# Swapping the banks of two accumulators, and tying two weight casts behind a copy, in the feed-forward of a two-layer trunk

## The chip, the cores and the metric

The kernel runs on one core of a Trainium2 chip. The metric is the device time of one execution in microseconds (us), lower is better. TensorE (PE) multiplies matrices into PSUM, ScalarE (ACT) and VectorE (DVE) work on SBUF and PSUM, and loads are issued by SyncE (SP) and GpSimd (POOL). Each engine takes its own instructions in order and waits for the others through semaphores.

## The reference

A trunk of two residual layers over 512 tokens of 1024 features in float32. Each layer adds a token mixer (layer 0 pools over windows, layer 1 is attention) and then a gated feed-forward; a last norm follows.

```python
for i in range(DEPTH):                                  # 2
    x = x + mixer_i(rmsnorm(x, norm_mix[i]))
    h = rmsnorm(x, norm_ffn[i])                         # (512, 1024)
    g = h @ ffn_w_gate[i]                               # (512, 2816)
    u = h @ ffn_w_up[i]
    x = x + (silu(g) * u) @ ffn_w_down[i]
return rmsnorm(x, norm_final)
```

## The kernel before

**Precision.** A float32 product is done in three passes of a narrower format. A weight tile is cast by ScalarE to its high part (`whi`, line 171), and VectorE subtracts it to get the rest (`wlo`, line 175). Tokens are held in the same two parts. A product is whi times the high tokens, whi times the low tokens, and wlo times the high tokens.

**Feed-forward by seven products.** The 2816 gate and up features are taken in groups of 256 of each, n = 0 to 10. A group is split by two into halves of features, of inputs and of tokens, and done with seven products (i = 0 to 6) of combined blocks where the plain way takes eight. `Group.product(i)` (line 696) gets the weights of product i, issues its matmuls, and then has the sums handled by `done` or `paired_done`. After the last of its products a group applies silu and multiplies gate and up (`gate_first`, line 767), and splits the result into parts `u_hi` and `u_lo` (`first_half`, `second_half`) for the down products. The down products (`Down`) are done in seven products too, for blocks of 3, 3 and 5 groups.

**Order of the work.** TensorE's order is written by hand in `PLAN`. Groups 0 and 1 go first, interleaved (`TWO`). Then come groups 2 to 10, the paired ones. Group 2's products go in the order 0, 2, 3, 1, 4, then product 0 of group 3, then 5 and 6 of group 2, and so on. From group 3 on, product 0 of a group is thus followed by products of other work, while group 2's product 0 is followed at once by its product 2. The order on ScalarE, VectorE and the load queues is chosen by a planner. It takes what is ready by its own reckoning, earlier program order first, and `high_priority` moves work forward. `issue_after(ins)` places an instruction behind `ins` on the same engine.

**Weights.** All weight operands of the kernel stand in one list, `queue`, in the order of their enqueuing; group 2's products 0, 1, 2, 3, 4 stand there in that order, followed by product 0 of group 3. `weights(i)` (line 151) issues loads up to five or ten operands ahead and casts and subtractions up to `split_ahead` operands ahead (four unless the caller says otherwise), as far as the five buffers of `whi` and `wlo` allow. Raw weights have five buffers (`wraw`) and three more for sums (`vraw`). Some operands are sums: a subtraction can be followed by VectorE additions (`then`, line 177) that form the raw weights of a later product. An entry `cast_behind` in an operand's item ties its cast (line 171) behind an instruction of ScalarE.

**PSUM banks.** There are eight. Groups 0 and 1 use four banks of the pool `mm` and four of the pool `ffps`, of which two belong to the sums p and two to the sums r. When product 6 of group 1 has been issued, both pools are closed and four tensors of two banks each take their place, `pair0` to `pair3`:

```python
fps.open("ffpairs", [P, 2, S], 1)
*A, Q, C = (fps.tile(f"pair{i}") for i in range(4))
```

`pair0` and `pair1` (A, used in turn by the groups) lie where `mm` was, `pair2` where p was, `pair3` where r was. An instruction that first writes a new tensor waits for the last reader of what lay there before.

**The copies.** Products 0, 2, 4 and 6 of a paired group go into its A tensor. After product 0 ScalarE copies A to Q (line 739, "first copy", kept as `self.kept`), so that product 2 can add to A while product 3 adds to Q. After product 2 it copies A to C (line 741), to which products 1 and 5 ("second products") add. Products 0, 2, 3, 5 and 6 have eight matmuls of 512 columns and eight of 256; products 1 and 4 have 24 of 256. The last reader of p before the change of pools is line 793, in product 6 of group 1; the last reader of r is line 789, in its product 5.

Of the kernel before, what the change touches and what calls it, by code (L numbers as in the profile page):

```python
# [75 lines left out]
def trunk_kernel(ctx: ExitStack, tc: tile.TileContext, x_in, xT, gam, gains, consts, ident_d, w0, wT, w1, wv, w_down, out):  # L76
# [37 lines left out]
    queue = []  # L114
# [26 lines left out]
    def load_sums():  # L141

        done = loaded["v"]
        for i in range(len(ready), min(len(queue), len(ready) + 20)):
            if queue[i]["kind"] == "v" and "src" in queue[i] and i not in raws:
                if "v" not in pools or len(done) >= V_TILES and queue[done[-V_TILES]]["last"] >= len(ready):
                    return
                load(i)
                done.append(i)

    def weights(i, split_ahead=4, load_ahead=5, held=0):

        load_ahead = queue[i].get("ahead", load_ahead)
        for n in range(loaded["w"], min(len(queue), i + load_ahead)):
            if queue[n]["kind"] == "w":
                load(n)
            loaded["w"] = n + 1
        load_sums()
        while len(ready) < min(loaded["w"], i + split_ahead):
            item = queue[len(ready)]  # L160
            if item["kind"] == "v" and "v" not in pools:
                break
            if "pool" not in item and len(ready) > i and held + sum("pool" not in it for it in queue[i : len(ready)]) >= RING:
                break
            shape = item["shape"]
            n = math.prod(shape)
            raw = raws[item.get("into", len(ready))]
            hi, lo = (pools.get(item.get("pool"), wspl).tile([P, 1024], F32R, name=item.get("pool", "w") + part) for part in ("hi", "lo"))
            if len(ready):
                with tc.issue_after(item["cast_behind"]) if "cast_behind" in item else nullcontext():  # L170
                    nc.scalar.copy(hi[:, :n], raw[:, :n])  # L171
            else:
                nc.vector.tensor_copy(hi[:, :n], raw[:, :n])
            with tc.issue_after(item["behind"]) if "behind" in item else nullcontext():
                nc.vector.tensor_sub(lo[:, :n], raw[:, :n], hi[:, :n].bitcast(F32))  # L175
            for into, more in item.get("then", ()):
                nc.vector.tensor_add(raws[into][:, :n], raws[into][:, :n], raws[more][:, :n])  # L177
            if "loads" in item:
                into, src = item["loads"]
                nc.gpsimd.dma_start(raws[into][:, :n].rearrange("p (k c) -> p k c", k=shape[0]), src, accum_op=ALU.add)  # L180
            if len(shape) == 2:
                ready.append(tuple(t[:, :n].rearrange("p (k m) -> p k m", k=shape[0]) for t in (hi, lo)))
            else:
                ready.append(tuple(t[:, :n].rearrange("p (g k m) -> p g k m", g=shape[0], k=shape[1]) for t in (hi, lo)))
        got = ready[i]
        ready[i] = None
        return got
# [280 lines left out]
    with ExitStack() as pctx:  # L468
# [5 lines left out]
        held = ExitStack()  # L474
# [20 lines left out]
        for c in range(NC):  # L495

            pieces = (slice(0, P), slice(P, S)) if c == 0 else (slice(0, S),)
            if c < 2 or c % 2 == 0:
                if c < 2:
                    load_x(c, pieces[0])  # L500
                whi, wlo = weights(j_in[0][c if c < 2 else 1 + c // 2], 1, 1)
# [7 lines left out]
            k = 0 if c < 2 else c % 2  # L509
# [98 lines left out]
    def ffn(layer, norm, third, nxt):  # L608
# [7 lines left out]
        gu, dn = j_ffn[layer]  # L616
        with ExitStack() as fctx:
# [19 lines left out]
            fps = Sums()  # L637
# [21 lines left out]
            held = ExitStack()  # L659
# [3 lines left out]
            class Group:  # L663
# [30 lines left out]
                    split(hi[:, 2:7, :], lo[:, 2:7, :], lst[:, 3:8, :])  # L694

                def product(self, i, held=0):
                    whi, wlo = weights(gu[self.n][i], held=held)
                    right = RIGHT[i]
                    if self.pairs:
                        a, q, c = self.pairs  # L700
                        to = (a, c, a, q, a, c, a)[i]
                        places = [(g, k) for g in range(2) for k in range(4)]
                        mat = lambda o, w, m, **kw: nc.tensor.matmul(o, lhsT=w, rhs=m, skip_group_check=True, **kw)  # L703
                        own = lambda g: to[:, g, HALVES[i == 1]]
                        if i in (1, 4):
                            for g, k in places:
                                mat(own(g), whi[:, g, k, :], right[:, 0, k, :], start=False, stop=False)
                                mat(own(g), whi[:, g, k, :], right[:, 1, k, :], start=False, stop=False)
                                mat(own(g), wlo[:, g, k, :], right[:, 0, k, :], start=False, stop=k == 3)
                        else:  # L710
                            for g, k in places:
                                both = to[:, g, :].rearrange("p (z c) -> p z c", z=2)
                                mat(both, whi[:, g, k, :], right[:, :, k, :], start=i == 0 and k == 0, stop=False)
                            for g, k in places:
                                mat(own(g), wlo[:, g, k, :], right[:, 0, k, :], start=False, stop=k == 3)
                        with tc.high_priority(URGENT if i < 5 else 100):
                            self.paired_done(i)
                        return
                    if i == 3:
                        self.sums["q"] = by_g(mm.tile())  # L720
                    elif i < 2:
                        self.sums["pr"[i]] = by_g(fps.tile("pr"[i]))
                    ps = self.sums["prpqprp"[i]]
                    for g in range(2):
                        for c in range(4):
                            for k, (w, z) in enumerate(((whi, 0), (whi, 1), (wlo, 0))):
                                nc.tensor.matmul(  # L727
                                    ps[:, g, :], lhsT=w[:, g, c, :], rhs=right[:, z, c, :],
                                    start=i in (0, 1, 3) and g + c + k == 0, stop=c == 3 and k == 2, skip_group_check=True,
                                )  # L730
                    with tc.high_priority(URGENT if i < 5 else 100):
                        self.done(i)
# [139 lines left out]
            groups = {0: Group(0, ct_common), 1: Group(1, ct_tile(hn, "ct_second"))}  # L872
# [4 lines left out]
            for at, (kind, n, i, *zs) in enumerate(PLAN[:-4]):  # L877
                if at in (0, 2):
                    b = 2 + at // 2
                    if b == 2:  # L880
                        late_banks[b] = third
                        norm.prepare(3, COLS)
                    else:
                        late_banks[b] = [r_tile(), by_four(mm.tile())]
                        for half in range(2):
                            norm.turn(b, half, late_banks[b][half])
                    late(b, 1)
                if at in (4, 6, 8):
                    for b in (2, 3):
                        late(b, at // 2)  # L890
                if kind == "down":
                    if n not in downs:
                        downs[n] = Down(n, A[0], C, Q)
                        A.reverse()
                    downs[n].product(i, *zs)
                    continue
                if kind == "quad" and i == 0:
                    groups[n] = Group(n, ct_common, (A[0], Q, C))
                    A.reverse()
                elif i == 0 and n not in groups:  # L900
                    groups[n] = Group(n, ct_common)
                groups[n].product(i, held={1: -2, 2: 1, 3: 1}.get(i, 0) if kind == "quad" else 0)
                if (n, i) == (2, 0):
                    with tc.high_priority(100), tc.issue_after(groups[2].kept.ins):
                        groups[1].second_half()
                    held.close()
                    late_u.append(open_pool("ffb", 2))
                if (n, i) == (1, 6):
                    fps.close()
                    mm.close()  # L910
                    fps.open("ffpairs", [P, 2, S], 1)
                    *A, Q, C = (fps.tile(f"pair{i}") for i in range(4))
                    A.reverse()


# [64 lines left out]
        return norm  # L980

    norm = ffn(0, norm, third, 1)


    with ExitStack() as actx:
# [179 lines left out]
        for t in range(8):  # L1165
# [4 lines left out]
            k = rope(pk, t, "k")  # L1170
# [115 lines left out]
        for part in range(2):  # L1286
            at = VA + part * VB
            pv = [mm.tile([P, S], F32, name="mm") for _ in range(4)]
            for c in range(4):
                whi, wlo = weights(j_v[part][c])  # L1290
# [137 lines left out]
```

## Time and profile before

| | |
|---|---|
| median of 3 runs | 990.42 us (990.29, 990.42, 991.89) |
| the profiled execution | 992.42 us, its span 990.6 us |
| TensorE busy | 975.5 us, 98% of the span |
| VectorE busy | 785.5 us, 79% |
| ScalarE busy | 580.5 us, 59% |
| mean granted TensorE clock | 0.991 |

The span is the time from the first to the last record of the execution. Rows of a timeline give the start, the duration, the engine, the line of the kernel, the operation, output<-inputs and the shapes; in square brackets stands the idle time of the engine before it and what ended it. "x8" joins eight instructions to one row. Instructions of one engine overlap by some tens of ns in the rows, so that the distance from one start to the next (the pitch) is shorter than the duration. A row of stretches gives the busy time of TensorE, its weight loads, VectorE, ScalarE and GpSimd, then the granted TensorE clock, the DMA share and GB/s.

### The profile page before, as it was taken

The page shows a single profiled execution, that of the slowest core. Times are in us where ns is not written, and L with a number is a line of the kernel's source. Part 1 is how long each engine was busy: PE and PEld are TensorE (multiplying, and loading weights), DVE is VectorE, ACT ScalarE, POOL GpSimd, SP SyncE. Part 2 cuts the span into 40 slices and gives each one's busy share as a digit, 9 for nine tenths or more (in the row PEclk, how much of TensorE's full clock was granted, in tenths as well). Part 3 has the DMA queues.
Part 4 walks back from the last instruction along what each step waited for, and adds up shares of the span by engine and source line. Part 5 has one row for each costly group of instructions (what it writes and reads, how often), then busy time and mean ns, then how long its engine had stood idle before and what let it go on. Part 6 is the DMA issues. An engine that isn't in the chain of part 4 may idle for free.

```text
span 990.6 us, 15451 instructions
## 1 busy us (share of the span) xinstructions
PE 975.5 (98%) x5948; PEld 862.3 (87%) x5948; DVE 785.5 (79%) x1085; ACT 580.5 (59%) x909; POOL 124.8 (13%) x124
## 2 busy tenths in 40 slices
PE   9999998999999999999999999999899999999997
PEld 8888897988988998889888899899788998899886
DVE  6485798897888888697897557589789798888876
ACT  5563665655665666574553554467564676567655
POOL 0002010011011111101211124101001101111110
PEclk9999998999999999999999999999899999999999
DMA  9448275379668876655221249617547956987652
GB/s 333 182 164 197 43 203 151 113 197 241 171 149 214 228 206 150 126 192 162 85 78 54 62 154 279 121 64 204 133 128 200 253 138 156 247 225 191 142 135 107
DMA packets 79465, 162.98 MB, mean 165 GB/s; under 512 B 6096, under 2 KB 6480, under 8 KB 79392
## 3 DMA queue, kind: packets, MB, share of 16 engines
q1 hardware_dynamic: 58544, 122.04, 37.3%
q0 software_dynamic: 20560, 39.69, 23.6%
q8 instruction: 46, 0.75, 0.3%
q14 instruction: 27, 0.22, 0.1%
q10 hardware_dynamic: 288, 0.27, 0.1%
HBM read 159.85 MB, written 2.13 MB: 164 GB/s over the span
## 4 chain that ended last, share of the span: by engine, by line
PE 96%; DVE 3%; ACT 1%; issue 0%; ACTq 0%
PE pair L703 36%; PE pair L845 21%; PE mm L264 5%; PE mm L266 4%; PE mm L265 4%; PE p L727 3%; PE early L515 2%; PE mm L425 2%; PE mm L427 2%; PE mm L426 2%; PE r L727 2%; PE mm L727 1%; PE mm L1296 1%; PE mm L1298 1%; PE mm L1297 1%; PE early L562 1%
## 5 line engine op out<-in xcount | busy, mean ns | idle before, releaser
L175 DVE TENSOR_TENSOR wlo<-wraw,whi 128x1024 fp32r<-128x1024 f32 (+2 forms) x190 | 221.7, 1172 | 68.7 <-ACT whi L171 68.2
L171 ACT CAST whi<-wraw 128x1024 fp32r<-128x1024 f32 (+2 forms) x189 | 183.9, 979 | 137.5 <-PE pair L703 29.1
L171 ACT CAST whi<-vraw 128x1024 fp32r<-128x1024 f32 (+1 forms) x108 | 105.2, 980 | 124.0 <-PE pair L703 40.9
L175 DVE TENSOR_TENSOR wlo<-vraw,whi 128x1024 fp32r<-128x1024 f32 (+1 forms) x108 | 121.5, 1133 | 56.9 <-ACT whi L171 52.2
L703 PE MATMUL pair<-h,whi 128*128 128x512 f32 (+1 forms) x720 | 161.1, 349 | 0.0
L703 PEld LDWEIGHTS pair<-h,whi 128*128 128x128 f32 x720 | 122.7, 189 | 15.0
L703 PE MATMUL pair<-t,whi 128*128 128x512 f32 (+1 forms) x576 | 128.0, 344 | 7.7 <-ACT pair L739 7.7
L703 PEld LDWEIGHTS pair<-t,whi 128*128 128x128 f32 x576 | 98.8, 194 | 18.2 <-ACT pair L739 8.1
L845 PE MATMUL pair<-wlo,u_hi 128*128 128x512 f32 (+1 forms) x284 | 110.0, 387 | 0.0
L845 PE MATMUL pair<-whi,u_hi 128*128 128x512 f32 (+1 forms) x284 | 109.9, 387 | 0.0
L845 PE MATMUL pair<-whi,u_lo 128*128 128x512 f32 (+1 forms) x284 | 109.8, 386 | 0.0
L703 PE MATMUL pair<-h,wlo 128*128 128x256 f32 x576 | 100.3, 281 | 0.0
L703 PEld LDWEIGHTS pair<-h,wlo 128*128 128x128 f32 x576 | 85.6, 188 | 4.7
L703 PE MATMUL pair<-t,wlo 128*128 128x256 f32 x432 | 82.2, 287 | 0.0
L138 POOL DMA_DIRECT2D wraw<-w x22 | 26.6, 1211 | 395.2 <-DMA wraw<-w 141.5
L177 DVE TENSOR_TENSOR vraw<-vraw,wraw 128x1024 f32<-128x1024 f32 (+1 forms) x66 | 75.2, 1139 | 0.7
L703 PEld LDWEIGHTS pair<-t,wlo 128*128 128x128 f32 x432 | 68.4, 195 | 3.1
L264 PE MATMUL mm<-h,whi 128*128 128x512 f32 (+1 forms) x176 | 64.3, 365 | 0.0
L265 PE MATMUL mm<-h,whi 128*128 128x512 f32 (+1 forms) x176 | 63.4, 360 | 0.0
L266 PE MATMUL mm<-h,wlo 128*128 128x512 f32 (+1 forms) x176 | 63.4, 360 | 0.0
L845 PEld LDWEIGHTS pair<-whi,u_lo 128*128 128x128 f32 x284 | 53.3, 188 | 10.9
L845 PEld LDWEIGHTS pair<-wlo,u_hi 128*128 128x128 f32 x284 | 53.4, 188 | 10.6 <-DVE wlo L175 0.3
(347 smaller groups left out, 1894.2 us busy)
## 6 DMA issues: line engine op xcount, KB each, us to landing
wraw<-w SPq DMA_DIRECT2D x116, 512.0 KB, 4.8
wraw<-w_down SPq DMA_DIRECT2D x32, 512.0 KB, 3.7
vraw<-w SPq DMA_DIRECT2D x22, 512.0 KB, 4.9
wraw<-w POOLq DMA_DIRECT2D x22, 512.0 KB, 6.0
vraw<-w POOLq DMA_DIRECT2D x22, 512.0 KB, 9.1
wraw<-wT SPq DMA_DIRECT2D x16, 512.0 KB, 4.5
vraw<-w_down POOLq DMA_DIRECT2D x12, 512.0 KB, 7.5
wraw<-w_down SPq DMA_DIRECT2D x24, 256.0 KB, 3.2
```

The costliest lines, as they stand in the source:

```text
L138: nc.gpsimd.dma_start(dst, more, accum_op=ALU.add)
L171: nc.scalar.copy(hi[:, :n], raw[:, :n])
L175: nc.vector.tensor_sub(lo[:, :n], raw[:, :n], hi[:, :n].bitcast(F32))
L177: nc.vector.tensor_add(raws[into][:, :n], raws[into][:, :n], raws[more][:, :n])
L264: nc.tensor.matmul(ps, lhsT=whi, rhs=xhi, start=first, stop=False, **kw)
L265: nc.tensor.matmul(ps, lhsT=whi, rhs=xlo, start=False, stop=False, **kw)
L266: nc.tensor.matmul(ps, lhsT=wlo, rhs=xhi, start=False, stop=last, **kw)
L425: nc.tensor.matmul(ps, lhsT=xhi, rhs=w[0][:, k, :], start=first, stop=False)
L426: nc.tensor.matmul(ps, lhsT=xhi, rhs=w[1][:, k, :], start=False, stop=False)
L703: mat = lambda o, w, m, **kw: nc.tensor.matmul(o, lhsT=w, rhs=m, skip_group_check=True, **kw)
L727: nc.tensor.matmul(ps[:, g, :], lhsT=w[:, g, c, :], rhs=right[:, z, c, :], start=i in (0, 1, 3) and g + c + k == 0, stop=c == 3 and k == 2 ...
L845: nc.tensor.matmul(acc(t), lhsT=u, rhs=w, start=first, stop=n == len(places) - 1, skip_group_check=True)
```

## The change

The tensors Q and C swap their places, so that Q is `pair3` and C is `pair2`. Product 0 of group 2 asks for operands three ahead and not four, so that the cast of product 3's weights is traced after the first copy of that group. The casts of the weights of products 3 and 4 of group 2 get a `cast_behind` on that copy. All of it is done in both layers.

```diff
                 def product(self, i, held=0):
-                    whi, wlo = weights(gu[self.n][i], held=held)
+                    whi, wlo = weights(gu[self.n][i], 3 if (self.n, i) == (2, 0) else 4, held=held)
...
                 if (n, i) == (2, 0):
+                    for k in (3, 4):
+                        queue[gu[2][k]]["cast_behind"] = groups[2].kept.ins
                     with tc.high_priority(100), tc.issue_after(groups[2].kept.ins):
                         groups[1].second_half()
                     held.close()
...
                     fps.open("ffpairs", [P, 2, S], 1)
-                    *A, Q, C = (fps.tile(f"pair{i}") for i in range(4))
+                    *A, C, Q = (fps.tile(f"pair{i}") for i in range(4))
                     A.reverse()
```

## The prediction

> **What bounds the kernel now.** I read the page's busy shares first, then who TensorE waits for, then the place of that wait engine by engine, and last the granted clock around it.
>
> ```profile
> PE 975.5 (98%) x5948; PEld 862.3 (87%) x5948; DVE 785.5 (79%) x1085; ACT 580.5 (59%) x909; POOL 124.8 (13%) x124
> ...
> PE pair L703 <- ACT pair L739: 7.7, 2, 3.8
> ...
> L739 ACT COPY pair<-pair x18: 997/1002/1013, 161.4 to 914.0; 128x1024 f32<-128x1024 f32 x18
> ...
>   DVE ct_second L793: 3.3, 2
> ```
>
> TensorE is the bound, 98% of the span. The list of waits shows one wait inside the work: 7.7 us in two pieces of up to 3.8 us, for the first copy (L739). There are 18 such copies, nine to a layer; only two are waited for, and the last row (idle time before L739) says these two themselves waited for VectorE's L793. They are group 2's, the first whose product 2 follows its product 0 directly. The timeline of the first layer, TensorE and then ScalarE:
>
> ```profile
> 155.62 2.02 PE L703 MATMUL pair<-h,whi 128*128 128x512 f32 x8
> 157.48 1.10 PE L703 MATMUL pair<-h,wlo 128*128 128x256 f32 x8
> 162.42 3.78 PE L703 MATMUL pair<-t,whi 128*128 128x512 f32 x8 [3.83 <-ACT pair L739]
> ...
> 167.69 2.02 PE L703 MATMUL pair<-h,whi 128*128 128x512 f32 x8
> ...
> 184.59 2.00 PE L703 MATMUL pair<-t,whi 128*128 128x512 f32 x8
> ...
> 187.38 2.02 PE L703 MATMUL pair<-h,whi 128*128 128x512 f32 x8
> ```
>
> ```profile
> 155.75 1.06 ACT L171 CAST whi<-wraw 128x1024 fp32r<-128x1024 f32 x1 [1.14 <-issue]
> 156.70 0.61 ACT L387 CAST u_hi<-ct_second 128x512 fp32r<-128x512 f32 x1
> 157.22 1.26 ACT L387 CAST u_hi<-ct 128x1280 fp32r<-128x1280 f32 x1
> 158.39 0.37 ACT L792 ACTIVATE ct_second<-p 128x256 f32<-128x256 f32 x1
> 158.66 1.03 ACT L171 CAST whi<-wraw 128x1024 fp32r<-128x1024 f32 x1
> 161.37 1.00 ACT L739 COPY pair<-pair 128x1024 f32<-128x1024 f32 x1 [1.67 <-DVE ct_second L793]
> ```
>
> Product 0 of group 2 runs from 155.62 to 158.58 (157.48 + 1.10). Product 2 needs the copy of its result and starts at 162.42. ScalarE itself stood idle for 1.67 us before that copy. VectorE says why:
>
> ```profile
> 151.71 0.69 DVE L789 TENSOR_TENSOR ct_second<-r,ct_second 128x512 f32<-128x512 f32 x1
> ...
> 156.59 1.22 DVE L175 TENSOR_TENSOR wlo<-wraw,whi 128x1024 fp32r<-128x1024 f32 x1
> 157.72 0.68 DVE L388 TENSOR_TENSOR u_lo<-ct_second,u_hi 128x512 fp32r<-128x512 f32 x1
> 158.32 1.22 DVE L177 TENSOR_TENSOR vraw<-vraw,wraw 128x1024 f32<-128x1024 f32 x1
> 159.46 1.48 DVE L388 TENSOR_TENSOR u_lo<-ct,u_hi 128x1280 fp32r<-128x1280 f32 x1
> 160.86 0.42 DVE L793 SCALAR_TENSOR_TENSOR ct_second<-p,ct_second 128x256 f32<-128x256 f32 x1
> ```
>
> VectorE runs without a break, and L793, last reader of p (group 1), comes at the end of its queue: done at 161.28, the copy starts at 161.37. The copy's target Q lies in p's banks. The last reader of r, L789, was done at 152.40. Second layer, the same place:
>
> ```profile
> 697.11 1.10 PE L703 MATMUL pair<-h,wlo 128*128 128x256 f32 x8
> 702.04 3.78 PE L703 MATMUL pair<-t,whi 128*128 128x512 f32 x8 [3.83 <-ACT pair L739]
> ...
> 707.17 2.02 PE L703 MATMUL pair<-h,whi 128*128 128x512 f32 x8
> ...
> 698.29 1.03 ACT L171 CAST whi<-wraw 128x1024 fp32r<-128x1024 f32 x1
> ...
> 700.99 1.00 ACT L739 COPY pair<-pair 128x1024 f32<-128x1024 f32 x1 [1.67 <-DVE ct_second L793]
> ```
>
> The gap costs more than itself. Product 2 takes 5.27 us (162.42 to 167.69) and in the second layer 5.13 (702.04 to 707.17); the same product of group 3 takes 2.79 (184.59 to 187.38). The stretches with the granted clock (the 1.00, 0.83, 0.50 in the third column from the end) show it:
>
> ```profile
> 160.50:161.00 0.50, 0.00 (x0) 0.00 (x0) 0.50 (x2) 0.00 (x0) 0.00 (x0) 0.83 0.66 127
> ...
> 162.40:167.70 5.30, 5.28 (x17) 4.51 (x18) 2.97 (x4) 2.31 (x2) 1.20 (x1) 0.50 0.69 163
> ...
> 167.50:168.00 0.50, 0.50 (x4) 0.46 (x4) 0.04 (x1) 0.11 (x1) 0.00 (x0) 0.85 1.13 209
> ...
> 700.00:700.50 0.50, 0.00 (x0) 0.00 (x0) 0.50 (x2) 0.00 (x0) 0.00 (x0) 0.63 0.55 111
> ...
> 706.50:707.00 0.50, 0.50 (x4) 0.50 (x4) 0.00 (x0) 0.40 (x1) 0.00 (x0) 0.54 1.02 184
> ```
>
> A half-full stretch at 0.83 is 66% full clock and the rest half clock, so the clock fell at 160.83 (2.25 us after the last matmul) and at 700.13 (1.92 us after it), and came back at 167.65 and 706.96: 6.82 and 6.83 us at half clock.
>
> **The change part by part.**
>
> *The swap.* Q now lies in the banks of r, free since 152.40. Nothing of the copy's target is late any more; it is bound by product 0's end (158.58) and its place on ScalarE. C moves onto p's banks; its first writer is L741, after product 2, so L793 then has until about 162.5. L793 is VectorE's next work after u_lo, so done by 161.3 even if nothing moved. Cost nothing.
>
> *The cast of product 3's weights* is traced one step later (three operands ahead of product 0, not four) and tied behind the copy; *the cast of product 4's* (155.75) is tied behind it too. Out of ScalarE's work ahead of the copy go two casts of 1.05. Out of VectorE's go the subtraction at 156.59 and the sum at 158.32, pitches of 1.13 and 1.14, and the subtraction for product 4 cannot start early. They come back after the copy.
>
> *The copy's new start.* u_hi at 156.70 needs L683, which runs ahead of anything removed, so I leave the two u_hi and L792 where they stand at the latest, and the copy takes the place at 158.66 where the third cast (the next group's operand 0) starts now. Ends: 158.62 if ScalarE is free when product 0 ends (the wait on TensorE costs it 0.04), and 159.61 if the third cast, which is not tied, still goes first (pitch about 0.95). I take 158.66 because the copy has the highest priority among what can start then. From the copy's start to product 2 are 1.05 us (161.37 to 162.42): product 2 at 159.71, a gap of 1.13 us. Saved: 161.37 − 158.66 = 2.71, second layer 700.99 − 698.29 = 2.70; together 5.41, with ends 5.5 and 3.5.
>
> *The clock.* If a gap of 1.13 us leaves the clock full, product 2 takes 2.79: saved 5.27 − 2.79 = 2.48 and 5.13 − 2.79 = 2.34, together 4.82. If not, see below. The bounds are 4.82 and, with the clock at half for two full windows, −2.0 (see the first rival).
> [...]
>
> *What is late next.* Product 3 would start at 159.71 + 2.79 = 162.50 and its low part 1.86 later, 164.36. After the copy (done 159.6) ScalarE has the rest of group 1's u_hi (pitch 1.17, as at 157.22) and then the cast of product 3's weights (1.05): done by 161.9, 0.6 to spare. VectorE then has u_lo (1.49) from 160.9 and the subtraction (1.22): done by 163.6, 0.8 to spare. Product 4's weights are needed after products 3 and 1, some 2.8 each, at about 168.1. I cost this at nothing; if the cover is gone, some tenths each layer. VectorE gets the two removed operations (2.27 us) back in this stretch; the second row below shows 2.39 us of idle time there to take them. The other rows are for the next part:
>
> ```profile
> 164.07 1.49 DVE L388 TENSOR_TENSOR u_lo<-ct_second,u_hi 128x1280 fp32r<-128x1280 f32 x1 [0.19 <-ACT u_hi L387]
> ...
> 167.96 1.23 DVE L175 TENSOR_TENSOR wlo<-vraw,whi 128x1024 fp32r<-128x1024 f32 x1 [2.39 <-PE pair L703]
> ...
> 159.60 0.37 SPq L136 DMA_DIRECT2D wraw<-w  x1
> ...
> 163.58 1.20 POOL L138 DMA_DIRECT2D wraw<-w  x1 [17.24 <-DMA wraw<-w]
> ...
> 181.07 1.05 ACT L171 CAST whi<-wraw 128x1024 fp32r<-128x1024 f32 x1 [0.77 <-PE pair L703]
> ...
> wraw<-w POOLq DMA_DIRECT2D x22, 512.0 KB, 6.0
> ```
>
> *The transfers.* The sum at 158.32 is the last reader of product 3's raw weights; its end (159.54) lets SP issue the load at 159.60 into that buffer, and POOL adds the second half 4.0 us later. With the sum ended near 164.8 the load issues then, POOL's at about 169, landed at 175 by POOL's median of 6.0 us. The operand (group 3, product 4) is cast at 181.07, on the new clock about 175.9, and multiplied some 12 us later. Behind it in SP's queue stands only the next load, a weight of the down products, needed later still. Nothing.
>
> *The end of the first layer.* Attention's first transposes go to the banks that Q now holds, whose last reader is later than C's:
>
> ```profile
> 445.76 0.68 DVE L388 TENSOR_TENSOR h<-pair,h 128x512 fp32r<-128x512 f32 x1
> ...
> 450.72 1.03 PE L358 MATMUL tp<-ident,wraw 128*128 128x128 f32 x8
> ```
>
> Free at 446.44, needed at 450.72: nothing.
>
> The sum: 5.41 + 4.82 = 10.23 us. The profiled execution has 992.42 us, a span of 990.6 and 1.8 around it; it becomes 982.2. It lies 2.0 above the median of 990.42, which becomes 980.2.
>
> **The rivals.**
>
> *The clock falls all the same.* For it: the falls came with 1.92 and 2.25 us of idle time in a window of 3.41 (half of 6.82), and no row shows what a third of a window does. Against: it is 0.6 of the smallest gap that did it. A fall followed by one full busy window costs half of 3.41 = 1.71 a layer: saved 5.41 + 4.82 − 3.42 = 6.8, or 983.6. Two windows at half clock would give 980.2 + 6.8 = 987.0.
> [...]
>
> *The third cast goes first.* Copy at 159.61, gap 2.08: saved 3.5 + 4.82 = 8.3, or 982.1 with the clock held. For it: this cast runs ahead of the copy today. Against: today the copy could not start then.
>
> *The swap frees nothing*, because the banks of the closed pool come free together. Then the copy waits for L793, which moves up by the two operations removed, 2.27, if u_lo is early enough: 160.86 − 2.27 + 0.51 = 159.10, saved 2 × 2.27 + 4.82 = 9.4, or 981.1; if u_lo only follows its cast of 157.22 (done 158.48), L793 starts at 159.9 and the copy at 160.4, saved 2 × 1.0 with the clock lost, 988.4.
>
> *Slower: the tied cast comes late.* Today a layer loses 3.83 (gap) + 2.41 (clock, the mean of 2.48 and 2.34). If product 3 waits w for its weights, soon after the gap of 1.13, both idle times can lie in one window, the clock falls for two windows (3.41), and 1.13 + w + 3.41 passes 6.24 at w = 1.70: the cast ending after 164.2, or its subtraction after 166.1. At w = 3 that is 2.6 us more, 993.0. For it: the slack is only 0.6 to 0.8. Against: it needs 2.3 us of work ahead of the cast beyond what is listed there.
>
> **How the numbers follow.** Forecast 0.65 (979.2 to 981.2); third cast first 0.13 (981.2 to 982.6); clock falls 0.11 (982.6 to 987); swap frees nothing 0.05 (981 to 988.4); slower 0.06, of which 0.03 end within 0.2% (2 us, about what a measurement of this kernel can tell from no change). The fourth's upper end counts 0.01 there too. So faster 0.93, same 0.04, slower 0.03. The range of 979.2 to 984.0 holds the first two, the third's lower price (983.6) and half of the fourth.
>
> **What would show it.** In the changed profile the list of waits has L703 on L739 with about 1.1 us twice; L739 is released by TensorE, not L793; the two casts stand behind it; product 2 takes 2.8 us at a clock of 1.00; no new wait at product 3. The forecast is wrong if the clock row still shows a 0.50 near 161, if L171 or L175 releases TensorE, or if the copy stands behind another cast.

## The result and the profile after

The changed kernel takes 981.89 us (median of four executions, 981.83 to 982.00) against 990.48 us (990.29 to 991.89) before: 8.6 us less, a ratio of 0.991 with a 95% interval of 0.989 to 0.993. The profiled execution took 981.91 us with a span of 980.1 us, 10.5 us less than the profiled execution of before. The page's busy shares:

```profile
PE 970.2 (99%) x5948; PEld 858.2 (88%) x5948; DVE 785.4 (80%) x1085; ACT 579.7 (59%) x909; POOL 124.7 (13%) x124
```

The list of waits (total, times, longest):

```profile
PE pair L703 <- ACT pair L739: 2.2, 2, 1.1
```

The groups, with busy time, mean ns, and the idle time ahead and what ended most of it:

```profile
L739 ACT COPY pair<-pair 128x1024 f32<-128x1024 f32 x18 | 18.0, 1002 | 14.0 <-PE pair L703 14.0
```

The wait of 7.7 us is 2.2 us, two pieces of 1.1. All of the idle time ahead of the copies now ends with TensorE; L793 isn't named any more. The first layer's timeline on TensorE, ScalarE and VectorE:

```profile
155.51 2.02 PE L703 MATMUL pair<-h,whi 128*128 128x512 f32 x8
157.37 1.10 PE L703 MATMUL pair<-h,wlo 128*128 128x256 f32 x8
159.55 2.12 PE L703 MATMUL pair<-t,whi 128*128 128x512 f32 x8 [1.09 <-ACT pair L739]
...
162.46 2.02 PE L703 MATMUL pair<-h,whi 128*128 128x512 f32 x8
164.32 1.10 PE L703 MATMUL pair<-h,wlo 128*128 128x256 f32 x8
...
155.71 0.39 ACT L792 ACTIVATE ct_second<-p 128x256 f32<-128x256 f32 x1 [2.16 <-PE p L727]
155.99 0.61 ACT L387 CAST u_hi<-ct_second 128x512 fp32r<-128x512 f32 x1
156.50 1.26 ACT L387 CAST u_hi<-ct 128x1280 fp32r<-128x1280 f32 x1
158.50 1.00 ACT L739 COPY pair<-pair 128x1024 f32<-128x1024 f32 x1 [0.74 <-PE pair L703]
...
160.58 1.99 ACT L171 CAST whi<-wraw 128x1024 fp32r<-128x1024 f32 x2
...
163.62 1.06 ACT L171 CAST whi<-wraw 128x1024 fp32r<-128x1024 f32 x1
...
155.20 0.68 DVE L682 TENSOR_TENSOR ct_second<-ct_second 128x512 f32<-128x512 f32 x1
...
156.14 0.41 DVE L683 SCALAR_TENSOR_TENSOR ct_second<-ct_second 128x256 f32<-128x256 f32 x1
156.47 0.41 DVE L793 SCALAR_TENSOR_TENSOR ct_second<-p,ct_second 128x256 f32<-128x256 f32 x1
...
162.12 2.35 DVE L175 TENSOR_TENSOR wlo<-wraw,whi 128x1024 fp32r<-128x1024 f32 x2
```

Product 0 ends at 158.47 (157.37 + 1.10), the copy starts 0.03 us later and product 2 at 159.55. Product 3 follows product 2 by 2.91 us without idle time. The row that was not forecast is the first of ScalarE: L792, at 158.39 before, runs at 155.71, ahead of the two u_hi and right at the end of product 6 of group 1, and VectorE's L793 moves with it from 160.86 to 156.47. The second layer's timeline:

```profile
693.72 2.12 PE L703 MATMUL pair<-t,whi 128*128 128x512 f32 x8 [1.09 <-ACT pair L739]
...
696.63 2.02 PE L703 MATMUL pair<-h,whi 128*128 128x512 f32 x8
```

A stretch of 5 us behind the start of product 2 in each layer:

```profile
160.00:165.00 5.00, 5.00 (x30) 4.34 (x29) 4.47 (x5) 4.86 (x6) 0.00 (x0) 1.00 0.10 25
...
695.00:700.00 5.00, 5.00 (x33) 4.52 (x32) 4.76 (x4) 4.86 (x6) 0.00 (x0) 1.00 0.28 94
```

TensorE stands idle for 1.09 us in each layer. Behind the gap it is busy all the time, at a granted clock of 1.00.

### The profile page after: what moved, and what is told of

Its sections match the earlier page's. It is cut to its first block, busy times and chain, and to the rows that moved or that the text cites. A ratio compares the mean times of both kernels' runs of the same rounds, so it can differ in the third digit from the quotient of the medians.

```text
span 980.1 us, 15452 instructions
## 1 busy us (share of the span) xinstructions
PE 970.2 (99%) x5948; PEld 858.2 (88%) x5948; DVE 785.4 (80%) x1085; ACT 579.7 (59%) x909; POOL 124.7 (13%) x124
## 4 chain that ended last, share of the span: by engine, by line
PE 98%; ACT 1%; DMA 0%; DVE 0%; SPq 0%; issue 0%; ACTq 0%
PE pair L703 36%; PE pair L845 21%; PE p L727 5%; PE mm L264 5%; PE mm L266 4%; PE mm L265 4%; PE r L727 2%; PE mm L425 2%; PE mm L427 2%; PE early L515 2%; PE mm L426 2%; PE mm L727 1%; PE mm L1298 1%; PE mm L1300 1%; PE mm L1299 1%; PE early L562 1%
## 5 line engine op out<-in xcount | busy, mean ns | idle before, releaser
L703 PE MATMUL pair<-t,whi 128*128 128x512 f32 (+1 forms) x576 | 124.7, 338 | 2.2 <-ACT pair L739 2.2
L703 PEld LDWEIGHTS pair<-t,whi 128*128 128x128 f32 x576 | 96.7, 190 | 12.0 <-ACT pair L739 2.6
L845 PEld LDWEIGHTS pair<-whi,u_hi 128*128 128x128 f32 x284 | 53.4, 188 | 10.5
```

What stands on the lines that cost most here:

```text
L845: nc.tensor.matmul(acc(t), lhsT=u, rhs=w, start=first, stop=n == len(places) - 1, skip_group_check=True)
```

## The experiments

Three edits were made at once, and one row (L792) had moved that the prediction had left in place. The theory from the changed profile: the cast of product 4's weights (155.75 before) stood in ScalarE's queue ahead of the two u_hi and L792, and L793 came behind L792; tying that cast is the whole gain of the gap. What the cast itself waited for until 155.75 the profile does not name ("issue"). That it was its buffer, which product 6 of group 1 frees, is inferred: the last matmuls of that product with whi start at 155.26 and end at 155.66. The rival is the prediction's account: the swap frees the copy of L793.

**The swap alone.** Before, with only

```diff
-                    *A, Q, C = (fps.tile(f"pair{i}") for i in range(4))
+                    *A, C, Q = (fps.tile(f"pair{i}") for i in range(4))
```

> The banks are swapped, no cast is tied. Theory A (the banks decide: the first copy only waits for the last reader of what lay in its banks): the copy starts at about 158.66, the gap is 1.1 us twice, the time is that of the full change, 981.9. Theory B (ScalarE's order decides): the swap frees the copy of VectorE's L793, but the untied casts stay ahead of it on ScalarE and the copy starts one cast later, near 159.6; the gap is 2.1 us twice, which is 2 us more, 983.9 with the clock held, and up to 3.4 us a layer more where the clock falls.

Measured: 986.11 us (983.26 to 987.35) against 991.21, a ratio of 0.9946 (0.9933 to 0.9958). ScalarE, TensorE and VectorE in the profile of the swap alone:

```profile
155.80 1.06 ACT L171 CAST whi<-wraw 128x1024 fp32r<-128x1024 f32 x1 [1.13 <-issue]
156.76 0.61 ACT L387 CAST u_hi<-ct_second 128x512 fp32r<-128x512 f32 x1
157.28 1.26 ACT L387 CAST u_hi<-ct 128x1280 fp32r<-128x1280 f32 x1
158.45 0.37 ACT L792 ACTIVATE ct_second<-p 128x256 f32<-128x256 f32 x1
158.72 1.03 ACT L171 CAST whi<-wraw 128x1024 fp32r<-128x1024 f32 x1
159.65 1.01 ACT L739 COPY pair<-pair 128x1024 f32<-128x1024 f32 x1
...
160.72 3.68 PE L703 MATMUL pair<-t,whi 128*128 128x512 f32 x8 [2.08 <-ACT pair L739]
...
698.01 2.11 PE L703 MATMUL pair<-t,whi 128*128 128x512 f32 x8 [2.08 <-ACT pair L739]
...
160.92 0.42 DVE L793 SCALAR_TENSOR_TENSOR ct_second<-p,ct_second 128x256 f32<-128x256 f32 x1
```

The last row is VectorE's L793. The swap does free the copy from it: the copy now starts ahead of L793 and not behind it. But ScalarE is then what makes it late: the third cast goes first, and the gap is 2.08 us in both layers. With the swap alone the rival "the third cast goes first" is what happens.

**The ties alone, with the old banks.** Against the changed kernel:

```diff
-                    *A, C, Q = (fps.tile(f"pair{i}") for i in range(4))
+                    *A, Q, C = (fps.tile(f"pair{i}") for i in range(4))
```

> Both casts are tied, the banks are as before. Theory A: the copy still waits for L793, 988 to 990.4. Theory B: without the casts ahead of it L792 runs as soon as product 6 of group 1 ends (155.7) and L793 at 156.5, so that p's banks are free long before product 0 of group 2 ends at 158.5; gap 1.1 us twice and 981.9, as with the full change.

Measured: 982.46 us (981.48 to 984.11) against 991.21, ratio 0.9914 (0.9902 to 0.9927). The wait for the copy is 1.1 us twice, as in the changed kernel. The ties need no swap.

**Only the cast of product 4 tied, old banks.** The operands are asked for four ahead again. Against the changed kernel:

```diff
-                    whi, wlo = weights(gu[self.n][i], 3 if (self.n, i) == (2, 0) else 4, held=held)
+                    whi, wlo = weights(gu[self.n][i], held=held)
...
-                    for k in (3, 4):
+                    for k in (4,):
...
-                    *A, C, Q = (fps.tile(f"pair{i}") for i in range(4))
+                    *A, Q, C = (fps.tile(f"pair{i}") for i in range(4))
```

> Only the cast of product 4's weights (155.75 before) is tied, banks and the cast of product 3 as before. Theory A: no change, 988 to 990.4. Theory B in its narrow form (this one cast, which itself waits for its buffer until product 6 of group 1 has ended, holds L792 and so L793 behind it on ScalarE): gap 1.1 us twice, 981.9. If it takes both casts: in between, 983 to 988.

Measured: 982.30 us (981.97 to 983.04), ratio 0.9912 (0.9899 to 0.9925). Its list of waits has the line of the changed kernel, 2.2 us in two pieces of 1.1. Its timeline of ScalarE and VectorE:

```profile
155.57 0.38 ACT L792 ACTIVATE ct_second<-p 128x256 f32<-128x256 f32 x1 [1.21 <-PE p L727]
155.85 0.61 ACT L387 CAST u_hi<-ct_second 128x512 fp32r<-128x512 f32 x1
156.36 1.26 ACT L387 CAST u_hi<-ct 128x1280 fp32r<-128x1280 f32 x1
158.37 1.00 ACT L739 COPY pair<-pair 128x1024 f32<-128x1024 f32 x1 [0.74 <-PE pair L703]
...
156.34 0.42 DVE L793 SCALAR_TENSOR_TENSOR ct_second<-p,ct_second 128x256 f32<-128x256 f32 x1
```

One cast tied gives all of it: L793 is done at 156.76, before product 0 has ended, so it no longer matters in whose banks Q lies. The three ratios (0.991, 0.9914, 0.9912) cannot be told apart. Without the cast two things change on ScalarE: its 1.05 us are gone, and the planner's order is L792, u_hi, u_hi instead of u_hi, u_hi, L792. For L792 the rows of before give the shares: the cast takes 0.95 us (155.75 to 156.70) and the two u_hi 1.69 (156.70 to 158.39), together 2.64 of the 2.68 us by which L792 moved. So most of it is the order, and the cast's wait until 155.75 held L792 by nothing, as product 6 of group 1 ends only at 155.78 (155.50 + 0.28). L793 moved further because it is now placed directly behind L683 and no longer behind two u_lo, a subtraction and a sum. Why the planner changes the order, and which of the two moves L793 by how much, was not taken apart.

**The first copy in two halves**, in the changed kernel, group 2 only:

```diff
-                        self.kept = nc.scalar.copy(q, a)
+                        if self.n == 2:
+                            for g in range(2):
+                                self.kept = nc.scalar.copy(q[:, g, :], a[:, g, :])
+                        else:
+                            self.kept = nc.scalar.copy(q, a)
```

> The full change, and group 2's first copy is made in two halves, one bank each. The remaining gap of 1.09 us is the copy's own 1.00 us: the first half can start when the first bank of product 0 is complete, 0.5 us before its end, and product 2 starts with that bank. Expected: gap 0.1 to 0.2 us twice, 2.0 us less than the full change, 979.9. If dependencies go by the whole tensor: gap 1.2 us, 982.1.

Measured: 982.01 us (981.76 to 982.48), ratio 0.991 (0.9895 to 0.9924). What TensorE waits for (the halves are L741 in this kernel's numbering):

```profile
PE pair L703 <- ACT pair L741: 2.5, 2, 1.3
```

Its timeline of TensorE and ScalarE:

```profile
156.93 1.10 PE L703 MATMUL pair<-h,wlo 128*128 128x256 f32 x8
159.29 2.11 PE L703 MATMUL pair<-t,whi 128*128 128x512 f32 x8 [1.26 <-ACT pair L741]
...
158.06 1.17 ACT L741 COPY pair<-pair 128x512 f32<-128x512 f32 x2 [0.74 <-PE pair L703]
```

The first half starts only when the whole of product 0 has ended (158.03), and product 2 only after both halves (159.23). The first half reads one half of A only. By the kernel's order of matmuls product 0 completes it four matmuls before its end, some 0.5 us by an estimate from product 2, whose eight low matmuls take 0.95 us here (161.24 to 162.19). The order between the engines thus goes by the whole tensor here, and two copies take 0.17 us more than one.

**The clock alone.** Before, with fifteen more matmuls of 512 columns between product 0 and product 2 (their sums are not used), so that the gap is filled and not shortened:

```diff
                 if (n, i) == (2, 0):
+                    for k in range(15):
+                        nc.tensor.matmul(
+                            C[:, k % 2, :].rearrange("p (z c) -> p z c", z=2), lhsT=h_hi[:, k % 4, 0:P],
+                            rhs=RIGHT[0][:, :, k % 4, :], start=True, stop=True, skip_group_check=True,
+                        )
```

> The kernel before, with 15 extra matmuls of 512 columns between product 0 and product 2 of group 2 in both layers (some 3.4 us at full clock, into C's banks, which the second copy overwrites; their sums are used by nothing). They leave the copy and its wait for L793 where they are and take only the idle time of TensorE away. If the clock term is real and apart from the gap: product 2 starts at the same 162.4, with a rest of the gap of 0.3 us, and runs at full clock in 2.8 us; the time is less than before by the clock term alone, 4.8 us against an execution like the profiled one, and on the median by whatever the clock costs there, about 3 us. If the half clock came from something other than idle time: product 2 still takes 5 us and the time does not move.

Measured: 987.77 us (987.06 to 987.89) against 991.26 (989.95 to 992.61), ratio 0.9966 (0.9952 to 0.9979).

```profile
158.31 3.58 PE L905 MATMUL pair<-h 128*128 128x512 f32 x15
162.30 2.11 PE L703 MATMUL pair<-t,whi 128*128 128x512 f32 x8 [0.40 <-ACT pair L739]
```

Product 2 starts where it did (6.79 us after product 0, 6.80 before), and yet 3.5 us are saved: that is the clock's share on the medians. Against the slowest execution of before, 992.61, it is 4.8 us, the prediction's price. The profile of this run also lists 0.7 us of waits elsewhere on TensorE that the list of before does not have, so the share may be a few tenths more.

**A longer gap.** The changed kernel with a half copy ahead of the first copy of group 2:

```diff
                     if i == 0:
+                        if self.n == 2:
+                            nc.scalar.copy(q[:, 0, :], a[:, 0, :])
                         self.kept = nc.scalar.copy(q, a)
```

> The full change, with one more copy of half the tensor (0.57 us) ahead of group 2's first copy, which lengthens the gap from 1.09 to about 1.6 us in both layers; the half copy writes what the whole copy then writes again. 1.6 us is 47% of a window of 3.41. In the swap-only run 39% of a window idle left the clock full and 61% halved it. If the limit is half a window or more: the clock stays full in all executions and the time is 981.9 + 1.1 = 983.0. If it lies between 39 and 47%: those executions whose gap falls into one window lose some 1.7 us a layer, 983 to 986.5, spread by execution.

Measured: 983.53 us (982.72 to 984.67), ratio 0.9925 (0.9913 to 0.9938): 1.6 us more than the changed kernel, where the two longer gaps add 2 × 0.60 = 1.2; its profile also lists three new waits elsewhere, of 0.7, 0.6 and 0.2 us. Its timeline at the gap:

```profile
159.96 2.14 PE L703 MATMUL pair<-t,whi 128*128 128x512 f32 x8 [1.69 <-ACT pair L741]
```

Next come the window of 3.41 us in which the gap lies, the window after it, and the stretch at the kernel's end in which the clock falls. They place the grid: a clock of 0.72 puts that fall at 980.22. A window is taken as half of the 6.82 us that before spent at half clock; the swap alone shows a single one, from 160.80 to 164.22. The two falls of before, at 160.83 and 700.13, lie 539.30 us or 158 windows apart, which makes a window 3.4133 us. Two falls at the kernel's end agree: before falls again at 986.86 (986 to 987 ran at 0.93), 286.73 us or 84.00 windows after 700.13, and the swap alone at 980.00, 819.20 us or 240.00 windows after 160.80. So 161.03, 240 windows ahead of 980.22, is an edge.

```profile
157.62:161.03 3.41, 1.72 (x11) 1.32 (x10) 2.61 (x3) 2.69 (x4) 0.00 (x0) 1.00 0.00 0
161.03:164.45 3.42, 3.42 (x20) 2.98 (x19) 3.33 (x3) 3.33 (x5) 0.00 (x0) 1.00 0.00 0
...
980.00:980.50 0.50, 0.00 (x0) 0.00 (x0) 0.00 (x0) 0.00 (x0) 0.00 (x0) 0.72 0.91 344
```

Half a window idle (1.69 of 3.41) left the clock full (1.00 in the next window). The swap alone says the same from the other side. Its first gap lies in one window; its second is split by the grid (693.28 is 156 windows after the fall at 160.80):

```profile
157.39:160.80 3.41, 1.33 (x11) 1.08 (x9) 3.41 (x4) 3.27 (x4) 0.00 (x0) 1.00 0.07 11
160.80:164.22 3.42, 3.42 (x8) 2.68 (x9) 3.23 (x6) 1.26 (x1) 0.62 (x1) 0.50 0.60 178
693.28:696.69 3.41, 2.65 (x16) 2.14 (x14) 3.41 (x6) 3.41 (x5) 0.00 (x0) 1.00 0.05 17
696.69:700.10 3.41, 2.09 (x10) 1.76 (x11) 3.41 (x6) 1.27 (x2) 0.00 (x0) 1.00 0.47 154
```

Of the first window 61% was idle (3.41 − 1.33 = 2.08), and the next one ran at 0.50. The second gap, as long, left 22% and 39% idle in two windows, and the clock stayed.

**Product 0 of group 2 earlier.** In the kernel before, with no cast tied, it goes ahead of product 6 of group 1, so that work stands between the copy and product 2. For that the accumulators are opened in two steps, A's first tensor and Q where `mm` was (banks 4, 5 and 6, 7), the others after product 6. This kernel leaves out a part of its sums, probably where product 3 overwrites Q and does not add to it; no run shows the place. Number and size of TensorE's instructions are those of the changed kernel, so its times can be read. The main lines:

```diff
-    steps = TWO + first(2)
+    steps = TWO[:-1] + first(2) + TWO[-1:]
...
-                if (n, i) == (2, 0):
+                if (n, i) == (1, 5):
+                    mm.close()
+                    fpa.open("ffpairs", [P, 2, S], 1, side="right")
+                    A, Q = [fpa.tile("pair0")], fpa.tile("pair1")
+                if (n, i) == (1, 6):
+                    fps.close()
+                    fps.open("ffpairq", [P, 2, S], 1)
+                    C = fps.tile("pair2")
+                    A = [fps.tile("pair3")] + A
+                    groups[2].pairs = (A[1], Q, C)
...
```

> The kernel before, no cast tied, but product 0 of group 2 is put ahead of product 6 of group 1 in TensorE's order, with A and Q in the banks of the earlier pool and C with the other A in those of p and r. The first copy then runs beside product 6 of group 1 (2.9 us of TensorE's time). If the copy is what TensorE waits for: no gap between the products, 2 x 1.1 us less than the full change, 979.7. If VectorE, which is busy without a break there, is the real bound behind it: a new wait on a cast or a rest of 1 to 2 us a layer takes the gap's place, 982 or more.

Measured: 982.94 us (981.84 to 984.15), ratio 0.992 (0.9906 to 0.9933). The gap in the feed-forward is gone in both layers, but attention has a new wait, and the clock falls behind it. (Two more new waits, at L1336, add 1.1 us.) The new wait in the list:

```profile
PE mm L264 <- DVE r L343: 2.1, 1, 2.1
```

VectorE's timeline ahead of it:

```profile
440.63 0.68 DVE L871 TENSOR_TENSOR x<-x,pair 128x512 f32<-128x512 f32 x1
441.22 0.16 DVE L343 RECIPROCAL r<-v 128x1 f32<-128x1 f32 x1
```

The stretch of the window of 3.41 us with the wait, and one of 1 us behind it:

```profile
438.90:442.31 3.41, 1.32 (x10) 0.93 (x9) 3.29 (x8) 3.22 (x6) 0.00 (x0) 1.00 0.71 173
...
443.00:444.00 1.00, 1.00 (x7) 1.00 (x6) 0.61 (x4) 0.29 (x2) 0.00 (x0) 0.50 0.85 310
```

The list names L343. L871, which ends at 441.31 just ahead of it, is by the placement of the tensors the last reader of the banks in which attention's first tile lies; the tile's matmuls start at 441.45. Which of the two held them is tested next, by moving the tensors.

**The same with the two tensors exchanged**, and beside it, on the same chip, the changed kernel again. Against the kernel with the early product:

```diff
-                    A, Q = [fpa.tile("pair0")], fpa.tile("pair1")
+                    Q, A = fpa.tile("pair0"), [fpa.tile("pair1")]
+                    for z in range(2):
+                        nc.tensor.matmul(
+                            Q[:, z, :].rearrange("p (z c) -> p z c", z=2), lhsT=h_hi[:, z, 0:P],
+                            rhs=RIGHT[0][:, :, z, :], start=True, stop=True, skip_group_check=True,
+                        )
```

The two matmuls are there to make TensorE's later additions to Q add to the copied sums. That they are needed for it is the author's estimate; no run exchanges the tensors without them.

> The earlier run with group 2's product 0 moved ahead of product 6 of group 1 lost its gap in the feed-forward in both layers, but got a new wait of 2.1 us at the start of attention, because attention's first tile lay in the banks of the accumulator that is flushed last. Here the first accumulator and the target of the first copies change places once more (banks 6 and 7, and 4 and 5), and two matmuls of 512 columns in each layer start the target's banks afresh before the first copy. If the place of the late flush was the cause, the wait of 2.1 us is gone; the two gaps of 1.1 us of the changed kernel are gone too, and the four added matmuls cost 4 x 0.23 = 0.9 us: 2.2 - 0.9 = 1.3 us less than the changed kernel on the same chip, about 980.6 us. If it is not, the wait of attention stays or moves to its next tile and the time is that of the changed kernel or up to 1 us more, 982 to 983.

> The changed kernel once more, beside the run with the early product, so that the two share a chip. Every theory expects the time measured before: 981.9 us, by up to 1 us more where the clock's windows fall otherwise.

Measured: 980.32 us (979.70 to 981.25) and, for the changed kernel, 981.69 us (981.26 to 981.83), against 991.06 before; ratios 0.9889 (0.9874 to 0.9904) and 0.9903 (0.9886 to 0.9919). All that TensorE still waits for in the version with the early product (a wait at the kernel's start that was there in the changed kernel too):

```profile
PE mm L302 <- DVE odd_rows L296: 1.1, 1, 1.1
```

Its timeline, with the added matmuls, products 0 and 2, and the copy on ScalarE:

```profile
149.89 0.63 PE L909 MATMUL pair<-h 128*128 128x512 f32 x2
...
153.23 2.02 PE L704 MATMUL pair<-h,whi 128*128 128x512 f32 x8
...
158.91 2.00 PE L704 MATMUL pair<-t,whi 128*128 128x512 f32 x8
...
156.81 1.01 ACT L740 COPY pair<-pair 128x1024 f32<-128x1024 f32 x1
```

The wait of 2.1 us in attention is gone: the tile's matmuls now start at 440.28, ahead of L871 (not among VectorE's rows up to 441.44) and of L343 behind it, so the banks were the cause. The copy is done at 157.82, 1.09 us before product 2, which follows product 6 of group 1 without a gap. The medians differ by 1.37 us; 2.2 us of waits less 2 × 0.46 us of added matmuls (149.89 to the next row at 150.35) are 1.3. The executions of the two versions touch at 981.25 and 981.26, so the order of the two is likely, but its size rests on four executions each.

## Why the prediction was right, and where it was not

*The forecast of 980.2 us* was 1.7 us too low, and the range held the time. By its own bands, 981.89 belongs to the rival "third cast first" (981.2 to 982.6) and not to the forecast (979.2 to 981.2), though the profile shows that this rival did not happen: the cast is behind the copy. So the number alone would have pointed to the wrong account.

*The copy's start and the gap* were right in size: the copy 0.03 us after product 0 (0.08 said, with 0.04 as the lower end), a gap of 1.09 us (1.13 said). The gap's term is 2 × (3.83 − 1.09) = 5.48 us against 5.41.

*The step that failed* is "I leave the two u_hi and L792 where they stand at the latest", and with it "the swap" as the release of the copy. Its reason, "u_hi at 156.70 needs L683", was a misreading: in the changed kernel this u_hi starts at 155.99, ahead of L683 (156.14) and 0.11 us after the end of L682. What stood ahead of u_hi and L792 before was the cast of product 4's weights. L792 moved by 2.7 us and L793 by 4.4. The swap alone leaves a gap of 2.08 us; one tied cast without the swap leaves 1.1. That the forecast of 158.66 came out is luck: the place of the third cast and the end of product 0 (158.58), to which the copy is really bound, happen to lie 0.08 us apart.

*The third cast* stayed behind the copy (163.62), though not for the priority that I gave as the reason: with the swap alone the copy had the same priority, and the cast went ahead. Why it stays behind once the cast of product 4's weights is tied, no run shows.

*The clock.* The sign and the mechanism held: product 2 takes 2.91 us at a clock of 1.00 (2.79 said; its first eight matmuls take 2.12 us where those of group 3 took 2.00). The term was mis-sized: 4.82 said, 3.5 on the medians. On the two profiles it is 5.27 − 2.91 + 5.13 − 2.91 = 4.58 us, and with the gap's 5.48 it makes 10.1 of the 10.5 us between the spans; 0.4 is unaccounted for. On the medians it is only the 3.5 of the filled gap: 5.5 + 3.5 = 9.0 against the measured 8.6 (9.4 on the chip of the last pair). The failed inference is that the profiled execution's 2.0 us above the median would stay in the changed kernel. They were part of the cost that the change removed: that execution had two half windows after each gap, a mean clock of 0.991, and those of before on the chip with the filled gap run from 989.95 us at 0.995 to 992.61 at 0.991. The changed kernel's four lie within 0.17 us.

*What is late next.* Nothing, as said: product 3 starts at 162.46 after its cast (the first of the two from 160.58, done about 161.6), and its low part at 164.32 after its subtraction (the first of two from 162.12, done about 163.3). The slack was 0.8 and 1.0 us. Neither the loads nor the layer's end show a new wait on TensorE. The slower rival did not occur.

*The clock's rival* did not occur: gaps of 1.09 to 1.69 us left the clock at 1.00. With longer gaps the place on the grid counted beside the length: 2.08 us cost a window in one place and nothing in the other. The falls here came with 56% to 66% of a window idle (1.92 to 2.25 us). The rival's window of 3.41 us, and its one window at half clock for a fall with a busy window behind it, are what the runs show: half clock lasted from 160.80 to 164.22 in the swap alone, and from 442.30 to 445.72 in the first kernel with the early product (442 to 443 ran at 0.65, 445 to 446 at 0.64).

*"The swap frees nothing"* is right as a verdict on the swap in the changed kernel, where the ties alone give the same time, and wrong in its working. With the swap alone the copy starts at 159.65, ahead of L793, so the banks do not come free together; and with the casts tied L793 did not wait for u_lo.

## What to carry to other kernels

When an operation at the end of an in-order queue is late, look for the instruction in front of it that isn't needed yet; moving that one can be worth more than its own duration, because a planner may reorder what was behind it (here a cast of 1.05 us, and L792 moved by 2.7). Where a stall lowers the clock, price its removal on the median of executions, not on one profile, since the cost of the clock changes with where the windows fall (here 3.5 us on the medians and 4.58 on two profiles). The stall on the short copy was removed here by other work between its two neighbours, and not by halving the copy; the banks that this takes must be chosen by when their last readers finish, or the wait turns up elsewhere (2.1 us in attention).

## What the runs showed of the hardware

In these runs the clock is decided window by window. Falls came where 56%, 61% (twice) and 66% of a window of 3.41 us was idle (1.92, 2.08, 2.09 and 2.25 us), none at 22%, 39% or 49.5%. The way back asked for more: before, the window from 160.83 to 164.25 was busy from 162.42, 54% of it, and the clock stayed at 0.50; after a full window (160.80 to 164.22 in the swap alone) it came back to 1.00. A gap of 2.08 us thus cost one window at half clock or none, whichever way the grid fell, and the gap of 3.83 us cost two in the profile (6.82 us). This is the likely cause of the 2.7 us between executions of one unchanged kernel (989.95 to 992.61). The swap alone says the same: two of its six executions, with a mean clock of 0.998, take 983.3 and 984.3 us, the other four, with 0.996, take 986.1 to 987.4.
